# State-space scan: one wide exponential per chunk, with the tokens' numbers added by GpSimd

## The chip, the core and the metric

The kernel runs on one core of a Trainium2 chip. A core has five engines that run side by side, each with its own in-order queue: TensorE (PE, matrix products; PEld is its weight load), VectorE (DVE), ScalarE (ACT, activations), GpSimd (POOL), and SyncE (SP), which issues most transfers. They share the on-chip memory SBUF; matrix products land in PSUM, which PE, DVE and ACT reach. The metric is the device time of one execution in microseconds; the runs of the kernel before lie between 2413.68 and 2415.92 us.

## The reference, cut to what matters

The reference is one layer of a hybrid streaming encoder: one large input projection, a state-space branch (SSD) and an attention branch side by side, an output projection, and a convolutional feed-forward part. The change touches the scan of the state-space branch only:

```
acum = cumsum(dt * a_neg)                        # over the tokens of a chunk
seg = acum[:, :, None] - acum[:, None, :]        # token l minus token s
decay = exp(where(causal, seg, -inf))
xdt = xc * dt
cb = einsum('blgn,bsgn->blsg', cc, bc)
y = einsum('blsg,blsge,bsgep->blgep', cb, decay, xdt)
y = y + einsum('blgn,bgepn->blgep', cc, state) * exp(acum)
state = state * exp(acum[:, -1]) + einsum('blgn,blge,blgep->bgepn', bc, exp(acum[:, -1:] - acum), xdt)
```

There are 32 heads in 4 groups of 8, with 64 values a head and a state of 128. One stream of 1024 tokens and one of 64 tokens are computed together (1088 tokens). The kernel uses chunks of 128 tokens where the reference has 64, which gives the same result.

## The kernel before, in words

Everything is float32. Large matrix products are made of three products of rounded high and low halves (lines 170 to 172 in `product`); they are most of PE's work, before, during and after the scan.

The scan (function `scan`, with `ask`, `front`, `back`, `gated`, `normed`, `scaled`) runs over 4 groups and, in each, 9 chunks: eight of 128 tokens and one of 64 for the short stream, 36 steps. Step by step:

- `ask` (L1284, SP) loads a tile `bc` of 128 rows by 8 heads by 128 tokens: the cumulated decay exponents of the chunk's 8 heads, the same in every row. It has four buffers and is asked for two steps ahead.
- `front` prepares a chunk: ACT takes exp of `bc` into `e2` (L1294, two halves of 64 rows); PE transposes the inputs (`tr`, L1297) and makes the product `cb` (L1299, L1300); ACT copies that to `b_cb` (L1302); DVE scales the inputs into `xx` (L1306). Then GpSimd masks `bc` in place (L1307, the upper triangle gets -1e30), ACT takes eight exponentials, one a head, each with that head's number of the row's token (`nacum`, the negated cumulated exponent) as bias (L1309), and DVE multiplies the result with `cb` (L1310). In this tile a row is token s and a column token l, so the bias is one number a row and head.
- `back` uses it: PE multiplies the weights in `bc` with `xdt` (`yi`, L1318) and the state with the chunk's C (`ye`, L1324); DVE puts these together (L1325, L1326). The state moves on: GpSimd multiplies it with the chunk's decay (L1335), PE makes the update (`stp`, L1330), DVE adds it (L1337). The next chunk's `ye` needs that sum.
- After each span of three chunks the result is gated and normed (L1344 to L1362, DVE and ACT).

`scan` calls `front` for the next chunk before `back` for the present one. Between steps `fill` runs pieces of the `filler`: the rest of the input projection and the branch products, so that PE has the large products to do while the chain of small operations runs. A scheduler, which reorders instructions by priority and by its own estimate of durations, sets the final order on each engine; once built, that order is fixed, and an engine whose next instruction isn't ready waits.

Of the kernel before, what the change touches and what calls it, by code (L numbers as in the profile page):

```python
# [11 lines left out]
AF = mybir.ActivationFunctionType  # L12
ALU = mybir.AluOpType
# [76 lines left out]
def hybrid_layer(ctx: ExitStack, tc: tile.TileContext, xT, xt, prm, cst, rope, wvd, win, wbs, wba, wout, wup, wdn,  # L90
                 ckT, cv, st0, yT, kT, v, ssm, conv, ffn):
    nc = tc.nc
    V, S, G, PE = nc.vector, nc.scalar, nc.gpsimd, nc.tensor
    act = S.activation
# [166 lines left out]
    nacum, decs = (dq.tile([P, 9, 32], F32, name=n) for n in ("nacum", "decs"))  # L261
# [1003 lines left out]
    with (tc.tile_pool(name="sin", bufs=1) as sin, tc.tile_pool(name="sp", bufs=1) as sp,  # L1265
# [21 lines left out]
        def front(g, ch, o, bx, xs, bc):  # L1287
            L = P if ch < 8 else TS
            cs = slice(o, o + L)
            h8 = slice(8 * g, 8 * g + 8)  # L1290
            e2 = sp.tile([P, 4, P], F32, name="e2", tag="e2", bufs=3)
            for u in range(2):
                half = slice(64 * u, 64 * u + 64)
                act(e2[half, :, :L], bc.rearrange("p (j u) t -> p u j t", u=2)[half, u, :, :L], AF.Exp)  # L1294
            tr = psi.tile([P, 512], F32, name="tr", tag="tr")
            for j in range(4):
                PE.transpose(tr[:L, P * j : P * (j + 1)], xs[:, j, cs], ident)  # L1297
            cb = psi.tile([P, 512], F32, name="cb", tag="cb")
            PE.transpose(cb[:L, 0:P], bx[:, 0, cs], ident)  # L1299
            PE.matmul(cb[:L, P : P + L], bx[:, 0, cs], bx[:, 1, cs], start=True, stop=True)  # L1300
            b_cb = sp.tile([P, 2 * P], F32, name="b_cb", tag="b_cb", bufs=3)
            S.copy(b_cb[:L, : P + L], cb[:L, : P + L])  # L1302
            xx = sp.tile([P, 2, 8, 64], F32, name="xx", tag="xx", bufs=2)
            xdt, xw = xx[:, 0], xx[:, 1]
            tr3 = tr[:L].rearrange("p (e q) -> p e q", e=8).unsqueeze(1).to_broadcast([L, 2, 8, 64])
            V.tensor_tensor(out=xx[:L], in0=tr3, in1=dtt[:L, :, ch, h8].unsqueeze(3).to_broadcast([L, 2, 8, 64]), op=ALU.mult)  # L1306
            G.affine_select(bc[:L, :, :L], bc[:L, :, :L], [[0, 8], [1, L]], ALU.is_ge, -1e30, base=0, channel_multiplier=-1)  # L1307
            for e in range(8):
                act(bc[:L, e, :L], bc[:L, e, :L], AF.Exp, bias=nacum[:L, ch, 8 * g + e : 8 * g + e + 1])  # L1309
            V.tensor_tensor(out=bc[:L, :, :L], in0=bc[:L, :, :L], in1=b_cb[:L, P : P + L].unsqueeze(1).to_broadcast([L, 8, L]), op=ALU.mult)  # L1310
            return L, cs, bc, e2, b_cb, xdt, xw

# [65 lines left out]
        def scan():  # L1378
# [9 lines left out]
            def begin(n):  # L1388
                if n == len(steps):
                    return None  # L1390
                if n and n + 2 < len(steps):
                    asked.append(ask(*steps[n + 2]))
                i, g, c, w, o = steps[n]
                return front(g, (c + o) // P, o, *got[i], asked[n])
# [465 lines left out]
    for i in range(4 * len(DOWN)):  # L1860
        g, last = i // 4, i % 4 == 3 and i + 1 < 4 * len(DOWN)
# [125 lines left out]
```

## Time and profile before

| | us |
|---|---|
| median of three runs | 2413.91 |
| the profiled execution | 2411.51 |
| its span, from the first to the last instruction | 2409.7 |
| first and last mask of the scan (L1307) | 1130.1 and 1441.5 |
| first and last start of `yi` (L1318) | 1138.7 and 1467.0 |
| ACT busy in the eight small exponentials (L1309) | 87.2 |
| GpSimd busy in masks (L1307) | 44.2 |
| GpSimd busy in state products (L1335) | 46.9 |

The profile gives for each engine the time in which it executes something. A busy PE is not PE at its best, since products overlap and their ends are modelled. Rows of instruction groups read: line, engine, operation, output and inputs, shapes, count, then the time the group kept the engine busy, the mean of one in ns, and the idle time of the engine just before such instructions with what ended it. Rows of a timeline begin with start and duration in us. A wait is put down to what came last by the trace.

### The profile page before, as it was taken

The page shows a single profiled execution, that of the slowest core. Times are in us where ns is not written, and L with a number is a line of the kernel's source. Part 1 is how long each engine was busy: PE and PEld are TensorE (multiplying, and loading weights), DVE is VectorE, ACT ScalarE, POOL GpSimd, SP SyncE. Part 2 cuts the span into 40 slices and gives each one's busy share as a digit, 9 for nine tenths or more (in the row PEclk, how much of TensorE's full clock was granted, in tenths as well). Part 3 has the DMA queues.
Part 4 walks back from the last instruction along what each step waited for, and adds up shares of the span by engine and source line. Part 5 has one row for each costly group of instructions (what it writes and reads, how often), then busy time and mean ns, then how long its engine had stood idle before and what let it go on. Part 6 is the DMA issues. An engine that isn't in the chain of part 4 may idle for free. (4 is left out here: it accounts for less than half of the span.)

```text
span 2409.7 us, 48636 instructions
## 1 busy us (share of the span) xinstructions
PE 2373.4 (98%) x18649; PEld 2302.2 (96%) x18649; DVE 1729.4 (72%) x2938; ACT 1201.2 (50%) x2600; POOL 634.4 (26%) x689
## 2 busy tenths in 40 slices
PE   8999999999999999999999999999999999999998
PEld 8999999999999999999898889999899999999998
DVE  4678887646858768884898886647866667677765
ACT  6444454335656656665566664334443343353442
POOL 0032443320100000001223220012254455443444
PEclk9999999999999999999999999999999999999999
DMA  7873768526554444435978956663124324357876
GB/s 246 273 245 129 266 221 303 170 102 208 160 156 161 151 144 137 148 110 188 353 266 280 331 192 205 203 215 130 65 82 164 138 98 162 127 191 211 246 184 106
DMA packets 288170, 449.74 MB, mean 187 GB/s; under 512 B 35833, under 2 KB 178306, under 8 KB 287938
## 3 DMA queue, kind: packets, MB, share of 16 engines
q1 hardware_dynamic: 258594, 387.00, 48.6%
q0 software_dynamic: 11040, 26.34, 5.4%
q10 hardware_dynamic: 18304, 33.30, 3.7%
q8 instruction: 147, 2.41, 0.4%
q14 instruction: 85, 0.70, 0.1%
HBM read 294.03 MB, written 152.50 MB: 185 GB/s over the span
## 5 line engine op out<-in xcount | busy, mean ns | idle before, releaser
L170 PE MATMUL mm<-b,w_hi 128*128 128x272 f32 x1376 | 407.7, 296 | 0.0
L171 PE MATMUL mm<-b,w_hi 128*128 128x272 f32 x1376 | 405.8, 295 | 0.0
L172 PE MATMUL mm<-b,w_lo 128*128 128x272 f32 x1376 | 403.8, 294 | 0.0
L171 PEld LDWEIGHTS mm<-b,w_hi 128*128 128x128 f32 x1376 | 259.5, 189 | 5.9 <-issue 4.1
L170 PEld LDWEIGHTS mm<-b,w_hi 128*128 128x128 f32 x1376 | 259.3, 188 | 5.3 <-issue 2.7
L172 PEld LDWEIGHTS mm<-b,w_lo 128*128 128x128 f32 x1376 | 259.0, 188 | 5.2 <-issue 4.2
L1629 PE MATMUL mx<-m,w_hi 128*128 128x272 f32 x792 | 152.3, 289 | 2.5 <-DVE hb L1667 1.3
L420 DVE TENSOR_TENSOR wh<-w_f,wh 128x512 fp32r<-128x512 f32 (+1 forms) x156 | 149.7, 960 | 0.7 <-ACT wh L419 0.7
L1629 PE MATMUL mx<-n,wh 128*128 128x272 f32 x1056 | 141.7, 288 | 1.3 <-DVE u L1656 0.9
L1629 PEld LDWEIGHTS mx<-n,wh 128*128 128x128 f32 x1056 | 135.7, 188 | 1.7 <-DVE u L1656 1.2
L1132 ACT ACTIVATE p_t<-sc,mx 128x512 f32<-128x512 f32 (+6 forms) x144 | 106.0, 739 | 59.0 <-DVE mx L1123 33.0
L1629 PEld LDWEIGHTS mx<-m,w_hi 128*128 128x128 f32 x792 | 124.4, 188 | 2.9 <-DVE hb L1667 1.5
L170 PE MATMUL mx<-b,w_hi 128*128 128x272 f32 x416 | 123.4, 297 | 1.1 <-ACT w_hi L155 0.8
L172 PE MATMUL mx<-b,w_lo 128*128 128x272 f32 x416 | 121.6, 294 | 0.0
L563 POOL TENSOR_TENSOR ws<-w_f 128x512 f32<-128x512 f32 (+1 forms) x51 | 69.0, 1354 | 195.4 <-DMA w_f<-in_wdn_dram 84.2
L171 PE MATMUL mx<-b,w_hi 128*128 128x272 f32 x416 | 120.4, 290 | 0.0
L1009 DVE SCALAR_TENSOR_TENSOR cc<-pre,par,cc 128x544 f32<-128x544 f32 (+1 forms) x144 | 111.2, 772 | 8.2 <-ACT cc L1007 6.9
L156 DVE TENSOR_TENSOR w_lo<-w_f,w_hi 128x1024 fp32r<-128x1024 f32 (+1 forms) x74 | 92.5, 1251 | 33.9 <-ACT w_hi L155 33.7
L1629 PE MATMUL mx<-m,w_lo 128*128 128x272 f32 x396 | 114.2, 289 | 0.0
L1638 ACT ACTIVATE cc<-pre,par 128x544 f32<-128x544 f32 (+1 forms) x44 | 37.2, 846 | 150.0 <-DVE pre L1673 149.1
L419 ACT CAST wh<-w_f 128x512 fp32r<-128x512 f32 (+1 forms) x156 | 95.3, 613 | 26.1 <-POOL w_f L569 6.8
L155 ACT CAST w_hi<-w_f 128x1024 fp32r<-128x1024 f32 (+1 forms) x74 | 77.6, 1049 | 56.1 <-PE mm L171 30.3
(466 smaller groups left out, 7124.8 us busy)
## 6 DMA issues: line engine op xcount, KB each, us to landing
w_f<-in_win_dram SPq DMA_DIRECT2D x40, 512.0 KB, 3.9
w_f<-in_wup_dram SPq DMA_DIRECT2D x80, 256.0 KB, 2.6
w_f<-in_win_dram SPq DMA_DIRECT2D x76, 256.0 KB, 3.2
bc<-a_sc SPq DMA_DIRECT2D x32, 512.0 KB, 7.0
b<-y_sc SPq DMA_DIRECT2D x24, 544.0 KB, 8.2
h_sc<-hb SPq DMA_DIRECT2D x44, 272.0 KB, 2.1
ht<-h_sc SPq DMA_DIRECT2D x22, 544.0 KB, 4.6
t_sc<-ht SPq DMA_DIRECT2D x22, 544.0 KB, 3.0
```

What stands on the lines that cost most here:

```text
L155: S.copy(hi, w)
L156: V.tensor_tensor(out=lo, in0=w, in1=hi, op=ALU.subtract)
L170: PE.matmul(ps, a_hi, b_hi, start=i == 0, stop=False)
L171: PE.matmul(ps, a_hi, b_lo, start=False, stop=False)
L172: PE.matmul(ps, a_lo, b_hi, start=False, stop=i == n - 1)
L419: S.copy(hi, src)
L420: V.tensor_tensor(out=lo, in0=src, in1=hi, op=ALU.subtract)
L563: G.tensor_tensor(out=s1, in0=q21, in1=q22, op=ALU.add)
L1009: V.scalar_tensor_tensor(cc[:, :m], pre[:, i : i + m], cw(i), cc[:, :m], ALU.mult, ALU.add)
L1132: act(p_t[:n, :nk], sc[c][:n, :nk], AF.Exp, bias=mx[:n, c : c + 1], accum_out=dst)
L1629: PE.matmul(ps, w[x][:, c], b[y][:, k], start=start and k == i == 0, stop=k == 3 and i == 2, skip_group_check=not start)
L1638: act(cc[:, :n], pre[h][:, :n], AF.Identity, bias=col(O_FB + f), scale=cw(0))
```

## The change

GpSimd adds the tokens' numbers to the whole `bc` tile (all 8 heads, `nacum` broadcast over the columns) ahead of the mask, and ACT takes one exponential of the whole tile, without a bias. In the changed kernel the add is L1307, the mask L1308, the exponential L1309; the lines after it keep their numbers.

```diff
@@ front
             V.tensor_tensor(out=xx[:L], in0=tr3, in1=dtt[:L, :, ch, h8].unsqueeze(3).to_broadcast([L, 2, 8, 64]), op=ALU.mult)
+            G.tensor_tensor(out=bc[:L, :, :L], in0=bc[:L, :, :L], in1=nacum[:L, ch, h8].unsqueeze(2).to_broadcast([L, 8, L]), op=ALU.add)
             G.affine_select(bc[:L, :, :L], bc[:L, :, :L], [[0, 8], [1, L]], ALU.is_ge, -1e30, base=0, channel_multiplier=-1)
-            for e in range(8):
-                act(bc[:L, e, :L], bc[:L, e, :L], AF.Exp, bias=nacum[:L, ch, 8 * g + e : 8 * g + e + 1])
+            act(bc[:L, :, :L], bc[:L, :, :L], AF.Exp)
             V.tensor_tensor(out=bc[:L, :, :L], in0=bc[:L, :, :L], in1=b_cb[:L, P : P + L].unsqueeze(1).to_broadcast([L, 8, L]), op=ALU.mult)
```

The scheduler then places instructions anew from the start of the scan on. On GpSimd at the start of the scan (`state` times `decs` is the state product of L1335):

```order
 L1003 COPY conv_o<-pre 128x3
 L1004 COPY conv_o<-pre 128x3
-L1307 AFFINE_SELECT bc<-bc 128x1024 x3
-L1335 TENSOR_TENSOR state<-state,decs 128x512
-L1307 AFFINE_SELECT bc<-bc 128x1024
+L1307 TENSOR_TENSOR bc<-bc,nacum 128x1024 x2
+L1308 AFFINE_SELECT bc<-bc 128x1024 x2
+L1307 TENSOR_TENSOR bc<-bc,nacum 128x1024
+L1335 TENSOR_TENSOR state<-state,decs 128x512
+L1308 AFFINE_SELECT bc<-bc 128x1024
```

Two adds now stand ahead of the first mask, and a third add ahead of the first state product.

On ACT at the same place (`w_hi` and `gt` belong to the filler, the numbers only tell buffers apart):

```order
 L1294 ACTIVATE e_14122<-bc 64x512 x2
 L1302 COPY b_cb<-cb 128x256
-L1294 ACTIVATE e_14151<-bc 64x512 x2
+L1294 ACTIVATE e_14145<-bc 64x512 x2
 L155 CAST w_hi<-w_f 128x1024
 L970 COPY gt<-mx 128x272
-L1309 ACTIVATE bc<-bc,nacum 128x128 x8
-L1294 ACTIVATE e_14260<-bc 64x512 x2
-L1309 ACTIVATE bc<-bc,nacum 128x128 x3
-L1302 COPY b_cb<-cb 128x256
-L1309 ACTIVATE bc<-bc,nacum 128x128 x5
+L1294 ACTIVATE e_14248<-bc 64x512 x2
```

The third chunk's `e2` moves ahead of the first chunk's exponential. 

On PE shortly before the first `yi` (lines 170 to 172 are products of the filler):

```order
 L172 MATMUL mm<-b_920,w_lo 128x272
 L170 MATMUL mm<-b_920,w_hi 128x272
+L1299 MATMUL cb<-con,in 128x128
+L1300 MATMUL cb<-in 128x128
 L171 MATMUL mm<-b_921,w_hi 128x272
+L1324 MATMUL ye<-in,state 128x128 x2
+L1297 MATMUL tr<-con,in 128x128 x4
+L1324 MATMUL ye<-in,state 128x128 x2
+L1330 MATMUL stp<-xx,b_cb 128x512
```

The second chunk's `cb`, `ye` and `stp` move ahead of the first chunk's `yi`; products of the filler that stood there follow later. PE executes the same 1964 rows between its first and last row of the scan, before and after.

## The prediction

> **What bounds the kernel now.** I read the head of the page first, then the windows around the scan, then the waits of TensorE in them.
>
> ```profile
> span 2409.7 us, 48636 instructions
> PE 2373.4 (98%) x18649; PEld 2302.2 (96%) x18649; DVE 1729.4 (72%) x2938; ACT 1201.2 (50%) x2600; POOL 634.4 (26%) x689
> ```
>
> TensorE (PE) is busy for 98% of the span; all others have room on average. The change touches only the scan, so the average says little. The windows show that stage (columns: window, length, then busy time with instruction count for PE, PEld, DVE, ACT, POOL, then granted clock, DMA share, GB/s):
>
> ```profile
> 1100.00:1130.00 30.00, 29.96 (x234) 28.50 (x233) 11.48 (x20) 11.53 (x29) 1.13 (x2) 1.00 0.55 185
> 1130.00:1180.00 50.00, 50.00 (x421) 44.02 (x419) 37.12 (x44) 40.46 (x106) 18.31 (x15) 1.00 1.05 352
> 1280.00:1330.00 50.00, 48.11 (x395) 43.56 (x395) 42.86 (x62) 32.71 (x77) 14.31 (x10) 1.00 0.86 290
> 1380.00:1430.00 50.00, 48.65 (x413) 44.57 (x413) 42.42 (x51) 33.21 (x82) 13.05 (x11) 1.00 0.65 216
> 1500.00:1550.00 50.00, 49.16 (x388) 48.73 (x388) 35.91 (x77) 21.58 (x43) 0.00 (x0) 1.00 0.74 226
> 1127.00:1470.00 343.00, 339.76 (x2765) 304.35 (x2764) 284.85 (x372) 216.91 (x523) 90.78 (x68) 1.00 0.81 275
> ```
>
> Over the scan (last row) PE idles 343 - 339.8 = 3.2 us. DVE idles 58 us, ACT 126 us, POOL 252 us. The waits of PE from 1100 to 1500 us name what those 3 us are:
>
> ```profile
> PE yi L1318 <- ACT y L1328: 1.9, 1, 1.9
> PE tr L1297 <- DMA in<-x_sc: 0.7, 1, 0.7
> PE yi L1318 <- DVE y L1326: 0.6, 1, 0.6
> PE mx L170 <- ACT grs L1355: 0.3, 1, 0.3
> ```
>
> None of them is on an exponential or on GpSimd's mask. So PE's own work sets the time here, and a change to ACT and POOL moves the end only where it makes PE wait, or takes one of these waits away.
>
> **The change, part by part.** Source views of the lines it touches (min/median/max in ns), and one row for a wide pass over ACT:
>
> ```profile
> L1309 ACT ACTIVATE bc<-bc,nacum x288: 332/387/409, 1133.8 to 1445.1; 128x128 f32<-128x128 f32 x128, 64x64 f32<-64x64 f32 x16
> 1133.79 2.45 ACT L1309 ACTIVATE bc<-bc,nacum 128x128 f32<-128x128 f32 x8
> 1127.00:1470.00 343.00, 87.21 (x288) 1.00 0.81 275
> L155 ACT CAST w_hi<-w_f 128x1024 fp32r<-128x1024 f32 x17 | 17.8, 1044 | 11.3 <-PE mx L171 5.6 <-PE mm L171 5.6
> ```
>
> Exponentials. 288 small ones keep ACT busy for 87.2 us (third row: the same window, this line alone), 2.45 us for the eight of a full chunk. One pass over 128x1024 is not in the trace as an Exp; a cast of that shape takes 1.04 us. Two half-height Exps of 512 take 1.27 us together (row below), which is the upper bound; I take 1.05, since the cast has the very shape. So ACT loses 32 x 1.4 us and some 6 us for the four half chunks, about 51 us. That work lies beside PE's: ACT already idles for 126 us here, so it is worth nothing by itself.
>
> The add on GpSimd. There are 36 new tensor-tensor operations, 32 of 128x1024 and 4 of 64x512, with a broadcast operand, as the state product has at half the width:
>
> ```profile
> L1335 POOL TENSOR_TENSOR state<-state,decs x28: 1037/1047/3618, 1140.7 to 1454.3; 128x512 f32<-128x512 f32 x28
> L1335 POOL TENSOR_TENSOR state<-state,decs 128x512 f32<-128x512 f32 x28 | 42.3, 1512 | 96.5 <-DVE state L1337 77.4 <-ACT state L1333 17.4 <-PE ye L1324 1.8
> L1307 POOL TENSOR_SCALAR_AFFINE_SELECT bc<-bc x36: 652/1092/2132, 1130.1 to 1441.5; 128x1024 f32<-128x1024 f32 x32, 64x512 f32<-64x512 f32 x4
> ```
>
> Twice the width at the undisturbed 1.04 us is 2.1 us, at the mean of 1.51 us it is 3.0 us; these are the ends, and I take 2.5. POOL's work grows by 32 x 2.5 + 4 x 1.2 = 85 us, from 91 to 176 of 343 us: not the bound by sum. A chunk's path from the bc rows to the masked weights becomes 2.5 - 1.4 = 1.1 us longer. ACT's exponential waits for POOL as before; behind it in ACT's queue stand the b_cb copies and the evacuations of PSUM, which ACT's 51 freed us cover on the whole.
>
> PE. It executes the same rows in the scan, from the same first to the same last place, in another interleaving; the price is 0, and if a few groups were split more, a few tenths of a us.
>
> **What the new operation disturbs.** Here the 1.51 us mean against the 1.04 us median matters. Two rows each of POOL and DVE around 1270 us:
>
> ```profile
> 1270.30 1.09 POOL L1307 TENSOR_SCALAR_AFFINE_SELECT bc<-bc 128x1024 f32<-128x1024 f32 x1 [2.63 <-ACT e L1294]
> 1271.35 2.01 POOL L1335 TENSOR_TENSOR state<-state,decs 128x512 f32<-128x512 f32 x1
> 1261.52 0.61 DVE L1362 SCALAR_TENSOR_TENSOR y<-y,par,grs 128x384 f32<-128x384 f32 x1
> 1270.54 1.92 DVE L1310 TENSOR_TENSOR bc<-bc,b_cb 128x1024 f32<-128x1024 f32 x1
> L1310 DVE TENSOR_TENSOR bc<-bc,b_cb 128x1024 f32<-128x1024 f32 x32 | 40.5, 1265 | 9.8 <-ACT bc L1309 5.9 <-ACT b_cb L1302 3.8
> L1306 DVE TENSOR_TENSOR xx<-tr,dtt 128x1024 f32<-128x1024 f32 x32 | 38.9, 1216 | 5.3 <-PE tr L1297 3.4 <-DMA o_sc<-ol 1.8
> L156 DVE TENSOR_TENSOR w_lo<-w_f,w_hi 128x1024 fp32r<-128x1024 f32 x17 | 22.9, 1345 | 10.4 <-ACT w_hi L155 10.4
> L1362 DVE SCALAR_TENSOR_TENSOR y<-y,par,grs 128x384 f32<-128x384 f32 x32 | 21.0, 712 | 0.1
> L1344 DVE SCALAR_TENSOR_TENSOR y<-in,par,y 128x384 f32<-128x384 f32 x32 | 20.2, 690 | 0.1
> ```
>
> DVE's product of bc starts while POOL masks, and takes 1.92 us where the undisturbed shape (L1306, which reads PSUM) has 1.22: it lost 0.70 us, nearly what the mask had left (1271.39 - 1270.54 = 0.85). Then POOL's product starts within DVE's and takes 2.01 us for 1.04. So an operation of POOL and one of DVE that reads two operands from SBUF hold each other up. The groups show the toll: against 1.216 us, L1310 lost 32 x 0.05 and L156 17 x 0.13 us; against the 0.61 us row, L1362 and L1344 lost 32 x (0.10 + 0.08) us; together 9.6 us, and these are the largest groups of their kind, not all, so 10 to 18 us for POOL's 91 us. The add doubles POOL's time, and a longer operation holds longer: I take 25 us of new loss on DVE, with 10 as the lower end and 36 x 2.1 = 75 us (each add blocks for its whole length) as the upper. 25 of DVE's 58 idle us remain cover; 75 would not fit.
>
> The Trainium skill (SBUF — State Buffer, section "Who interferes with whom") says that a DVE instruction with two SBUF inputs contends with a GpSimd instruction that reads SBUF, and that the second to issue is blocked until the first ends, not slowed; these rows agree (0.70 of 0.85 us). By that rule at its worst the time is that of the third rival below; by the grouped rows it is the forecast.
>
> **Where it reaches PE.** In the first nine chunks the slack is shortest. Rows of ACT, PE and DVE:
>
> ```profile
> 1128.71 1.27 ACT L1294 ACTIVATE e<-bc 64x512 f32<-64x512 f32 x2 [1.01 <-DMA o_sc<-ol]
> 1131.27 1.27 ACT L1294 ACTIVATE e<-bc 64x512 f32<-64x512 f32 x2 [0.89 <-DMA bc<-a_sc]
> 1136.34 1.23 DVE L1310 TENSOR_TENSOR bc<-bc,b_cb 128x1024 f32<-128x1024 f32 x1 [0.34 <-ACT bc L1309]
> 1138.71 1.09 PE L1318 MATMUL yi<-bc,xx 128*64 128x128 f32 x16
> 1176.51 1.21 DVE L1310 TENSOR_TENSOR bc<-bc,b_cb 128x1024 f32<-128x1024 f32 x1
> 1178.93 1.09 PE L1318 MATMUL yi<-bc,xx 128*64 128x128 f32 x16
> 1145.23 0.68 DVE L1337 TENSOR_TENSOR state<-state,stp 128x512 f32<-128x512 f32 x1
> 1147.22 1.05 PE L1324 MATMUL ye<-in,state 128*128 128x128 f32 x8
> ```
>
> Chunk 0's weights are ready at 1137.57 and yi starts at 1138.71: 1.1 us to spare; chunk 6 has 1178.93 - 1177.72 = 1.2 us; the third chunk's ye has 1147.22 - 1145.91 = 1.3 us. Now POOL has add, add, mask, mask, add ahead of the first state product. From the end of ACT's e2 at 1130.0: adds end at 1132.6 and 1135.1, masks at 1136.2 and 1137.3, so chunk 0's weights are ready at 1136.2 + 1.05 + 1.2 = 1138.5. In the new order PE comes to yi about 1 us later than before (six products of 0.13 us fewer ahead of it, but cb, ye and stp of the next chunk more), 1139.8 by estimate: still 1.3 us to spare. The third add ends at 1139.8, the state product 1.0 to 1.7 us later, DVE's sum 0.7 us after that, at 1141.5 to 1142.2; PE comes to that ye after yi (1.1), cb (0.3) and two products, at about 1141.4. So ye waits 0.1 to 0.8 us; I take 0.7. This is the new wait: the state product now queues behind an add that it doesn't need, and what is late next is ye. The 25 us on DVE are 0.7 us a chunk; with some three chunks of the 36 that have only about 1 us to spare I put 3 x 0.7 = 2.1 us.
>
> **The sum.** The profiled execution took 2411.5 us (its span of 2409.7 and 1.8 around it). Add 0 for PE's work, 0 for ACT's 51 us, 0.7 for ye, 2.1 for late weights: 2414.3. The median of the runs shown is 2.4 us above this execution, so 2416.7, and I predict **2417 us**. Its own range is 2411 (no new wait, the 1.9 us wait gone) to 2419. About 0.2% (4.8 us) is what a measurement of this kernel can tell from no change.
>
> **The rivals.**
>
> Slower: POOL sets the pace. Mechanism: its queue is in order, and add, mask and state product of a chunk take 2.5 + 1.2 + 1.5 = 5.2 us, against a pace of (1178.9 - 1138.7) / 6 = 6.7 us in the first chunks. It decides once holds and waits for the previous state add 1.5 us a chunk. Against it: POOL's idle rows are waits for ACT and DVE that partly overlap this. For it: state products of up to 3.6 us, and 77 us of POOL's time waiting for DVE's state, behind which adds now queue. Price: nine chunks late by about 1.1 us each, 10 us: 2411.5 + 10 + 2.4 = 2424.
>
> Slower still: each add blocks DVE for its whole length. 75 us less 58 idle leaves 17 us for PE: 2431. Against it: the mean losses of DVE's groups are a tenth, not a whole operation.
>
> Faster: the freed ACT and the scan's earlier end take away all PE idle from 1100 to 1550 us: 3.2 in the scan and 0.8 in the window 1500 to 1550. 2413.9 - 4.0 = 2410. For it: the 1.9 us wait is on an ACT copy. Against it: that is all there is, so more than 4.8 us can hardly be won.
>
> The change does not do what it says: if one wide Exp takes 1.27 us or the mask goes slower on fresh sums, ACT still has room, and the time is that of the forecast.
>
> **How the numbers follow.** Forecast 0.52; POOL as the pace 0.33; full blocking 0.08; faster 0.07. The range is 2410 to 2428: it takes in the forecast, the first rival with 4 us above its price, and most of the faster case, and leaves out full blocking. Of the faster case a little over half lies beyond 0.2%, so faster 0.04, within 0.2% 0.55, slower 0.33 + 0.08 = 0.41.
>
> **What would show it.** ACT's group at L1309 should be 36 operations of about 1.05 us, ACT busy in the scan down by about 50 us. The add should be 36 operations with a mean near 2.5 us and a least value near 2.1. L1310, L1344, L1362 and L156 should have longer means, DVE busier by 10 to 40 us. PE's waits in the scan should name ye on DVE's state and yi on DVE's bc, each under 1 us, 6 us or less in all. I am wrong if PE's idle time in the scan exceeds 8 us, if the add's mean is over 3 us, or if PE's waits stand outside the scan.

## The result, and the profile after

The changed kernel takes 2429.2 us (median of six runs, 2427.6 to 2432.1), the kernel before 2414.3 us (six runs, 2410.8 to 2420.0). The ratio is 1.0061 with a 95% interval of 1.0048 to 1.0075: some 15 us slower, 12 us above the forecast of 2417 and 1.2 us above its range. The profiled execution's span is 2425.8 us, 16.1 more than before.

The head of the page after, and the windows around the scan (window, length, busy time with count for PE, PEld, DVE, ACT, POOL, then granted clock, DMA share, GB/s):

```profile
span 2425.8 us, 48419 instructions
PE 2379.5 (98%) x18649; PEld 2304.3 (95%) x18649; DVE 1759.3 (73%) x2938; ACT 1153.0 (48%) x2348; POOL 715.3 (29%) x725
```

```profile
1100.00:1130.00 30.00, 29.71 (x232) 28.24 (x232) 10.57 (x19) 11.49 (x29) 1.13 (x2) 1.00 0.51 171
1130.00:1180.00 50.00, 47.18 (x385) 40.91 (x384) 40.07 (x38) 27.18 (x45) 37.00 (x22) 1.00 1.05 345
1180.00:1230.00 50.00, 45.52 (x356) 41.30 (x356) 39.58 (x56) 21.90 (x33) 14.03 (x11) 0.97 0.86 293
1280.00:1330.00 50.00, 45.73 (x368) 40.02 (x369) 49.04 (x59) 25.81 (x39) 29.02 (x16) 1.00 0.76 245
1380.00:1430.00 50.00, 50.00 (x408) 45.06 (x406) 42.12 (x48) 26.42 (x44) 25.20 (x14) 1.00 0.78 264
1127.00:1487.00 360.00, 346.08 (x2770) 307.16 (x2770) 314.52 (x371) 169.55 (x272) 170.88 (x104) 1.00 0.80 263
```

The time went into the scan, in its first two thirds: PE idles 2.8, 4.5 and 4.3 us in the three windows of 50 us shown up to 1330 us, and nothing between 1380 and 1430. Over the scan (last row) PE idles 13.9 us, where it was 3.2. ACT fell from 216.9 to 169.6 us as worked out. GpSimd rose from 91 to 171 us. DVE rose by 30 us, though it has not one instruction more: 284.9 to 314.5. The window 1280 to 1330 has DVE at 49.0 of 50 us.

The waits of PE from 1100 to 1500 us (engine, place, what it waited for: total, times, longest):

```profile
PE mx L172 <- DVE w_lo L156: 4.1, 1, 4.1
PE gst L1352 <- DVE zin L1348: 1.8, 2, 1.0
PE cb L1299 <- ACT b_cb L1302: 1.5, 2, 1.1
PE ye L1324 <- DVE state L1337: 1.3, 1, 1.3
PE tr L1297 <- DVE y L1345: 1.2, 1, 1.2
PE yi L1318 <- DVE y L1326: 1.1, 1, 1.1
PE yi L1318 <- DVE bc L1310: 1.0, 2, 0.7
```

Six of the seven are on DVE, at six different lines: it is not one operation that grew, DVE is late in many places. Groups of DVE by shape in the scan, against those quoted before:

```profile
L1310 DVE TENSOR_TENSOR bc<-bc,b_cb 128x1024 f32<-128x1024 f32 x32 | 49.4, 1548 | 5.0 <-ACT bc L1309 4.2 <-ACT b_cb L1302 0.8
L1306 DVE TENSOR_TENSOR xx<-tr,dtt 128x1024 f32<-128x1024 f32 x32 | 38.8, 1213 | 1.9 <-DMA o_sc<-ol 1.9
L1344 DVE SCALAR_TENSOR_TENSOR y<-in,par,y 128x384 f32<-128x384 f32 x32 | 28.8, 957 | 0.1
L156 DVE TENSOR_TENSOR w_lo<-w_f,w_hi 128x1024 fp32r<-128x1024 f32 x17 | 25.1, 1476 | 7.1 <-ACT w_hi L155 7.1
L1362 DVE SCALAR_TENSOR_TENSOR y<-y,par,grs 128x384 f32<-128x384 f32 x32 | 23.3, 786 | 0.1
```

Of these five only those with two operands from SBUF are longer. L1306 reads one from PSUM and keeps its 1.21 us. Against the same marks as before (1.213 and 0.61 us) the four others lost 10.7, 11.1, 4.5 and 5.6 us, 31.9 together; it was 9.6. The timeline shows a single hold, POOL's rows first, then DVE's:

```profile
1168.59 2.60 POOL L1307 TENSOR_TENSOR bc<-bc,nacum 128x1024 f32<-128x1024 f32 x1
1171.14 1.35 POOL L1335 TENSOR_TENSOR state<-state,decs 128x512 f32<-128x512 f32 x1
1169.94 1.65 DVE L1348 TENSOR_TENSOR zin<-zin 128x384 f32<-128x384 f32 x1
1171.52 2.06 DVE L1310 TENSOR_TENSOR bc<-bc,b_cb 128x1024 f32<-128x1024 f32 x1
```

DVE's sum of 384 elements starts 1.25 us before the add ends, and ends 0.40 us after it: it hardly moved while the add ran.

### The profile page after: what moved, and what is told of

Read it like the earlier page. It is cut to its first block, busy times and chain, and to the rows that moved or that the text cites. A ratio compares the mean times of both kernels' runs of the same rounds, so it can differ in the third digit from the quotient of the medians.

```text
span 2425.8 us, 48419 instructions
## 1 busy us (share of the span) xinstructions
PE 2379.5 (98%) x18649; PEld 2304.3 (95%) x18649; DVE 1759.3 (73%) x2938; ACT 1153.0 (48%) x2348; POOL 715.3 (29%) x725
## 4 chain that ended last, share of the span: by engine, by line
PE 51%; DVE 4%; DMA 3%; issue 2%; POOL 1%; ACT 0%; SPq 0%; POOLq 0%; DVEq 0%; ACTq 0%
PE mx L1629 13%; PE mx L1803 6%; PE mm L1629 5%; PE mm L172 3%; PE mm L170 3%; PE mm L171 3%; PE mx L170 3%; PE mx L172 3%; PE mx L171 3%; PE mm L1803 2%; PE po L1167 1%; PE yi L1318 1%; PE ye L1324 1%; PE stp L1330 1%; DMA bc<-a_sc 1%
## 5 line engine op out<-in xcount | busy, mean ns | idle before, releaser
L1307 POOL TENSOR_TENSOR bc<-bc,nacum 128x1024 f32<-128x1024 f32 (+1 forms) x36 | 74.5, 2072 | 124.4 <-ACT e L1294 124.4
L1646 POOL TENSOR_TENSOR hb<-hb,cc 128x544 f32<-128x544 f32 (+2 forms) x63 | 67.1, 1079 | 133.7 <-DVE hb L1667 96.8
```

The source lines that it names most:

```text
L1307: G.tensor_tensor(out=bc[:L, :, :L], in0=bc[:L, :, :L], in1=nacum[:L, ch, h8].unsqueeze(2).to_broadcast([L, 8, L]), op=ALU.add)
```

## The experiments

Theories: **A**, GpSimd's add holds DVE's operations with two SBUF operands, DVE gets late, and PE waits for DVE. **B**, the scheduler's new order is itself worse. **C**, GpSimd's own queue is late: the longer path over add, mask and exponential, and the state product behind adds. Ratios are to runs of the kernel before on the same chip. In the last two columns stands the busy time of DVE and GpSimd, in us, from 1120 us to the end of the scan.

| kernel | ratio, 95% interval | about us | DVE | GpSimd |
|---|---|---|---|---|
| before | 1 | 0 | 287 | 91 |
| changed | 1.0061 (1.0048 to 1.0075) | +15 | 316 | 171 |
| wide_no_add | 1.0027 (1.0016 to 1.0038) | +7 | 287 | 86 |
| side_add | 1.0090 (1.0075 to 1.0106) | +22 | 322 | 171 |
| add_eight | 1.0099 (1.0083 to 1.0115) | +24 | 315 | 165 |
| add_dve | 1.0021 (1.0011 to 1.0031) | +5 | 326 | 99 |
| side_memset | 1.0005 (0.9996 to 1.0015) | +1 | 286 | 201 |
| after_state_dve | 1.0077 (1.0062 to 1.0092) | +19 | 328 | 132 |
| add_halves | 1.0079 (1.0063 to 1.0096) | +19 | 311 | 183 |
| state_dve | 1.0006 (0.9996 to 1.0017) | +1 | 296 | 43 |
| wide_memset | 1.0057 (1.0039 to 1.0076) | +14 | 289 | 162 |
| eight_no_add | 1.0045 (1.0031 to 1.0059) | +11 | 283 | 81 |
| two_no_add | 1.0015 (1.0005 to 1.0025) | +4 | 285 | 85 |
| side_copy | 1.0043 (1.0028 to 1.0058) | +10 | 310 | 181 |
| same_order_short | 1.0028 (1.0017 to 1.0039) | +7 | 286 | 95 |
| same_order_memset | 1.0033 (1.0021 to 1.0045) | +8 | 288 | 119 |
| memset_as_add | 1.0062 (1.0047 to 1.0077) | +15 | 309 | 209 |

### One part alone

The changed kernel without its add:

```diff
-            G.tensor_tensor(out=bc[:L, :, :L], in0=bc[:L, :, :L], in1=nacum[...], op=ALU.add)
             G.affine_select(bc[:L, :, :L], ...)
             act(bc[:L, :, :L], bc[:L, :, :L], AF.Exp)
```

> The changed kernel without GpSimd's add: the tokens' numbers are left out, so the decays are wrong; the wide exponential and the mask stay. Theory A (the add's hold on DVE's SBUF reads makes DVE late, and DVE makes PE late): DVE's loss falls back to its old level, PE idles 3 to 5 us in the scan, time within 0.2% of before (2410 to 2418). Theory B (the new order that the scheduler makes around one wide exponential is itself worse, by late weights for PE): still 2422 to 2430.

1.0027: between the two. DVE is back at 287 us, yet PE still waits 3.5 us for a `w_lo` and 3.0 us for ACT's copy of `grs`. So A does not cover all of it.

The kernel before with an add beside the path:

```diff
+            side_add = sp.tile([P, 8, 112], mybir.dt.bfloat16, name="side_add", tag="side_add")
+            G.tensor_tensor(out=side_add[:L, :, : min(L, 112)], in0=xx[:L]...[:, :, : min(L, 112)], in1=nacum[...], op=ALU.add)
             V.tensor_tensor(out=bc[:L, :, :L], in0=bc[:L, :, :L], in1=b_cb[...], op=ALU.mult)
```

> The kernel before (eight biased exponentials) plus one GpSimd add of 128x896 a chunk, from xx and nacum into a tile that nobody reads: the same kind of load on GpSimd, but not on the path from bc to the weights. Theory A (holding DVE up is what costs): 8 to 14 us slower than before, DVE's two-operand groups lose about as much as in the changed kernel. Theory C (the longer path from bc over add, mask and exponential to the weights is what costs): within 5 us of before.

1.0090, 22 us where A had said 8 to 14, and far from C's 5 us. The add need not be on the path to cost.

The changed kernel with narrow exponentials:

```diff
-            act(bc[:L, :, :L], bc[:L, :, :L], AF.Exp)
+            for e in range(8):
+                act(bc[:L, e, :L], bc[:L, e, :L], AF.Exp)
```

> The changed kernel with eight narrow exponentials in place of the wide one, without bias; the add on GpSimd stays. Theory A: the add does it, so 12 to 20 us slower than before, no faster than the changed kernel, since ACT's time is no bound. Theory B: order around the wide exponential is the cause, so within 5 us of before.

1.0099, 24 us where A had said 12 to 20. The add costs with narrow exponentials too; that A's figures are passed twice says that something adds to the holds (the section on order below).

The add on DVE:

```diff
-            G.tensor_tensor(out=bc[:L, :, :L], ...
+            V.tensor_tensor(out=bc[:L, :, :L], ...
```

> The changed kernel with the add on DVE instead of GpSimd: 36 more DVE operations of about 1.2 us (43 us), no new hold by GpSimd. DVE then has about 328 busy us of 343 in the scan. Theory A, which says that DVE's time is the scarce thing: 10 to 25 us slower than before, much like the changed kernel, since GpSimd's add costs DVE 27 us by holds. Theory C (GpSimd's queue, in order, is late): about as before, since GpSimd's queue is as it was.

1.0021: A's form that DVE's time as such is scarce fell. DVE is busy for 326 us, 10 more than in the changed kernel, and the kernel is 10 us faster than that one. C's forecast, about as before, was the nearer one; whether a full queue is the cause is asked next.

### What on GpSimd costs

The kernel before with memsets beside the path:

```diff
+            side_add = sp.tile([P, 8, 112], mybir.dt.bfloat16, name="side_add", tag="side_add")
+            G.tensor_copy(out=side_add[:L, 0, 0:1], in_=xx[:L, 0, 0, 0:1])
+            for _ in range(3):
+                G.memset(side_add[:L], 0.0)
             V.tensor_tensor(out=bc[:L, :, :L], in0=bc[:L, :, :L], in1=b_cb[...], op=ALU.mult)
```

> The kernel before plus, a chunk, three GpSimd memsets of a tile that nobody reads (and a one-column copy that ties them to the chunk): GpSimd's queue is about as full as with the add beside the path, but the memsets read nothing from SBUF. Theory A (the add holds DVE's two-operand reads): DVE's loss stays at 15 to 25 us and the time within 5 us of before. Theory C (GpSimd's queue gets late, whatever runs in it): 10 us slower or more, as with the add beside the path.

No change (1.0005, the interval holds 1), with the fullest GpSimd but one: 201 us. Its row in the scan, to be held against the last row of the profile after:

```profile
1127.00:1468.00 341.00, 338.86 (x2753) 302.79 (x2752) 284.64 (x370) 216.09 (x522) 201.20 (x212) 1.00 0.83 276
```

DVE has its old 284.6 us and PE idles 2.1 us. Here GpSimd's queue is more than twice as full without harm, with memsets, which read nothing from SBUF. The Trainium skill (SBUF — State Buffer, section "Who interferes with whom") says just that: a DVE instruction with two SBUF inputs contends with a GpSimd instruction that reads SBUF and not with one that only writes it. These runs agree.

The state product on DVE in the changed kernel, and in the kernel before:

```diff
-                G.tensor_tensor(out=new.rearrange("p (e q) -> p e q", e=8), in0=state.rearrange(...), ...
+                V.tensor_tensor(out=new.rearrange("p (e q) -> p e q", e=8), in0=state.rearrange(...), ...
```

> The changed kernel with the state product (L1335) on DVE, so that it no longer queues behind adds. Theory C: most of the 15 us come back, 2414 to 2420. Theory A: the adds still hold DVE and only the state product's own holds go; 5 to 15 us slower than before remain.

> The kernel before with the state product on DVE: 32 DVE operations of some 0.7 us more (22 us), GpSimd left with the masks. Theory A: DVE loses about 10 us less by holds, and the time is within 5 us of before, perhaps a little faster. If DVE's busy time as such were scarce: 5 to 15 us slower.

1.0077 and 1.0006. With nothing queued behind the adds but masks, the loss is still there: C's 2414 to 2420 falls. It is also above the 5 to 15 us that A had left. In the kernel before, 32 more operations on DVE cost nothing that can be measured, and the holds that they spare win nothing.

The add in two halves of four heads:

> The changed kernel with the add in two operations of four heads each: the same elements, holds of half the length. If the length of one hold does it: 2418 to 2424, DVE's longest products well under 2.9 us. If the sum of held time does it: 2426 to 2434, as the changed kernel.

1.0079, no better than one whole add: shorter holds were no remedy here. The two kernels differ in order too, so the 4 us between them can't be put down to the halves.

GpSimd copies that read one operand, beside the path:

```diff
+            for _ in range(2):
+                G.tensor_copy(out=side_add[:L, :, : min(L, 112)], in_=xx[:L]...[:, :, : min(L, 112)])
```

> The kernel before plus, a chunk, two GpSimd copies of 128x896 from xx to a tile that nobody reads: one operand read from SBUF where the add reads two. If any GpSimd read holds DVE: 8 to 20 us slower, DVE's loss 35 us or more. If only GpSimd's two-operand operations do: within 5 us of before, DVE's loss under 25 us.

1.0043, with DVE at 310 us for 287 before: one operand read is enough to hold DVE up.

### How much is order

> The changed kernel with the add replaced by two GpSimd memsets of a tile nobody reads, ahead of the mask (the tokens' numbers are left out, so the decays are wrong): about the same delay ahead of the mask, but nothing read from SBUF. Theory A (the add costs by holding DVE's reads): about the time of the kernel without the add, 2415 to 2421. Theory C (the delay ahead of the mask costs): 2426 to 2432.

> Eight narrow exponentials without bias and no add (the tokens' numbers are left out): the kernel before but for the bias. Theory B (the order made around one wide exponential costs some 6 us): within 3 us of before.

> Two exponentials of four heads each, no add (the tokens' numbers are left out). Theory B as a property of wide exponentials: 2 to 7 us slower than before, between eight and one. Theory B as chance (any new order may be some us better or worse): anywhere within 8 us of before, also outside those two.

(`wide_memset` puts a one-column copy of `bc` and two memsets of 128x896 where the add stood; the other two are the kernel without add with eight or two exponentials.)

1.0057, 1.0045 and 1.0015. A had wide_memset at the time without the add; that missed, and DVE's 289 us say that it isn't holds. C had it 12 to 18 us up, and 14 fit; but its order is new as well, and this run can't part a delay from an order. B's first forecast, within 3 us for eight_no_add, missed too. Without an add, eight, two and one exponential give +11, +4 and +7 us: in no order of width. So each of these changes made the scheduler place some 1600 products and the small operations anew, and such an order costs about 4 to 11 us by itself in the three kernels without an add.

To part order and holds, the order had to stay. In the next three the program is built as in a measured kernel, and only then, with all instructions and their waits in place, GpSimd's instruction in the add's place is replaced:

```diff
+    # in the finished program, for each GpSimd add bc <- bc, nacum:
+    b.instructions[k] = _short(i)                                  # same_order_short: one column
+    b.instructions[k] = _as(mybir.InstMemset, i, [], [i.outs[0]], ...)   # same_order_memset: memset of the tile
+    # memset_as_add, in side_memset's program: of three memsets of side_add
+    b.instructions[k] = _as(mybir.InstTensorTensor, i, [x, y], [o], op=ALU.add)   # the first: an add of 836, from par and nacum
+    b.instructions[k] = _short(i)                                  # the second: one column
```

> The changed kernel with every instruction in its place, but the add cut to one column (the tokens' numbers are left out): what is left against before is the new order alone. Theory A (holds make up most of the loss): 2 to 7 us slower than before. Theory B (the new order makes up most of it): 10 to 16 us slower, as the changed kernel.

1.0028: the changed kernel's order alone costs about 7 us. PE's waits in it:

```profile
PE tr L1297 <- DMA in<-x_sc: 2.4, 1, 2.4
PE mx L172 <- DVE w_lo L156: 2.4, 1, 2.4
PE cb L1299 <- ACT grs L1355: 1.8, 1, 1.8
PE cb L1299 <- ACT b_cb L1302: 1.6, 1, 1.6
```

The wait for `w_lo`, 4.1 us in the profile of the changed kernel, is 2.4 us here: more than half of it is there without the add.

> The changed kernel with every instruction in its place, but the add replaced by a memset of the same tile, about 1 us long and reading nothing (the weights become constants). Theory A: within 3 us of the kernel whose add is cut to one column. Theory C (delay ahead of the mask and of the state product): at least half way from that kernel to the changed one.

1.0033, with a memset of 0.95 us: the delay that it brings costs at most a us or so. It is half as long as the add, so it speaks for a delay of that length only. For the add's own delay there is the DVE row of L1310 above: DVE waited 4.2 us in all for the exponentials in the changed kernel, and 5.9 us before.

> The kernel before plus three memsets a chunk, every instruction in its place, but of each three memsets the first is now an add of 128x836 of two SBUF operands and the second is cut to one column: GpSimd's queue is about as full as with three memsets, the order the same. Theory A: DVE's loss rises from 18.6 to 35 us or more and the time by 8 us or more over before. If the order decides and holds don't: within 4 us of before, as with three memsets.

1.0062 against 1.0005 for the same order with memsets: some 14 us from adds in the place of memsets, in an order that costs nothing. Its row in the scan:

```profile
1127.00:1484.00 357.00, 343.98 (x2765) 305.76 (x2763) 307.10 (x371) 217.03 (x524) 209.31 (x212) 1.00 0.79 265
```

DVE is 22 us up on its twin with memsets, GpSimd's queue 8 us fuller, and PE idles 13.0 us for 2.1. The longest wait of PE is one for a load, and the trace leads it back to DVE: the load was issued only when DVE's `y` (L1348 there) was done, for which the issuing queue had waited 3.6 us.

```profile
SPq L1271 <- DVE y L1348: 3.6, 1, 3.6
1403.83 2.26 DVE y L1348 x3
1406.96 6.80 DMA in<-x_sc
PE tr L1297 <- DMA in<-x_sc: 3.6, 1, 3.6
```

GpSimd comes late as well in this run: DVE waits 6.0 us for it, where it is 0.3 us in the twin. So a part of the 14 us can be C's; in the changed kernel DVE has no such wait.

So of the changed kernel's 15 us, the order takes 1.0028, about 7 us, and what its add does in that order the rest, about 8 us; the intervals leave the first some 3 us either way and the second some 4. That the 8 us are holds in the main rests on DVE's busy time, which falls from 316 to 286 us when the add is cut away in this order, and on memset_as_add; that no part of them is the longer delay ahead of the mask is not shown. No version here beats the kernel before.

## Why the prediction failed

**The bound** was read rightly: PE's work set the time, and only waits of PE could move it.

**ACT** was right: 36 exponentials of 1.06 us (1.05 said), 47 us less work, worth nothing in time.

**The add** came near the lower end: a mean of 2.17 us for the 32 full ones, where 2.1 to 3.0 was the range and 2.5 the choice.

```profile
L1307 POOL TENSOR_TENSOR bc<-bc,nacum 128x1024 f32<-128x1024 f32 x32 | 69.4, 2170 | 110.4 <-ACT e L1294 110.4
L1307 POOL TENSOR_TENSOR bc<-bc,nacum x36: 1035/1898/4777, 1131.4 to 1461.8; 128x1024 f32<-128x1024 f32 x32, 64x512 f32<-64x512 f32 x4
L1309 ACT ACTIVATE bc<-bc x36: 630/1058/1063, 1138.5 to 1464.8; 128x1024 f32<-128x1024 f32 x32, 64x512 f32<-64x512 f32 x4
```

**DVE's loss** was right in mechanism and size: 25 us said, 30 more busy us measured, 22 of them in the four quoted groups.

**"PE ... the price is 0"** failed. The sum took the same rows in another interleaving as free. The same order with the add cut away costs 7 us: in the new order PE comes to a `w_lo`, a load or a copy of ACT before it is ready. The profile of before could not show that, and the orders printed ahead of the prediction show that rows move, not what it costs. Why this order is the worse one stays open.

**"With some three chunks of the 36 ... 3 x 0.7"** was mis-sized, the term "late weights". It put DVE's loss on the chunk's own weights alone, and its slack was measured in the first nine chunks alone, while the window from 1280 to 1330 has 4.3 of the 13.9 us in which PE idles. Even at the first chunk, where it had 1.3 us to spare, `yi` waits: two products of `bc` (L1310) take 4.86 us together there, where two undisturbed ones take 2.4.

```profile
1139.55 4.86 DVE L1310 TENSOR_TENSOR bc<-bc,b_cb 128x1024 f32<-128x1024 f32 x2 [0.95 <-ACT bc L1309]
1142.47 1.09 PE L1318 MATMUL yi<-bc,xx 128*64 128x128 f32 x16 [0.65 <-DVE bc L1310]
```

In the changed kernel `yi` waits for `bc` for only 1.0 us; PE waits for DVE at `w_lo`, `gst`, `tr`, `ye` and `yi`. What the add costs in its order is about 8 us, not the 2.1 and 0.7 of the sum. The step in error was "25 of DVE's 58 idle us remain cover": DVE still idles 45 us in the changed scan, and PE waits for it all the same, so idle time spread over the stage is no cover for an operation that is late where PE needs it. PE's idle time in the scan, 13.9 us, is past the 8 us that the prediction named as the sign of being wrong. In add_dve, some 45 us of added DVE work in place of the holds cost only 5 us; that the scheduler had placed that work is a likely reason, not a shown one.

**The new wait of ye** was right in its place: the third chunk's `ye` waits 1.3 us for DVE's `state`, and the state product had started when the third add ended; 0.7 us was said.

**The rivals.** GpSimd as the pace had a better time than the forecast (2424), but memsets that filled its queue to 201 us did nothing. Full blocking, 2431, was nearest to the measured 2429, and that is luck: a single hold can look as it said, but DVE lost 30 us and not 75, and some 7 of the 15 us are order, which it left out.

## What to carry to other kernels

Moving work to an idle GpSimd is not free where DVE works on two SBUF operands at the same time: look in the trace for DVE groups of one shape whose mean lies above their shortest, and count every GpSimd operation that reads SBUF against them. Holds can become waits of the engine that sets the time even where the held engine has idle time left; here the same work cost 5 us on the busier engine and 15 on GpSimd, each in an order of its own. And where a scheduler orders the program, treat the new order as a term of its own, with a spread taken from variants of the kernel (here 4 to 11 us), before a few us are put down to an operation.

## What the runs showed of the hardware

A wait of PE can cost more than its length. After the 4.1 us wait in the changed kernel the granted clock fell:

```profile
1185.00:1190.00 5.00, 3.73 (x24) 2.81 (x22) 5.00 (x5) 2.81 (x4) 3.17 (x3) 1.00 0.82 254
1190.00:1195.00 5.00, 1.78 (x11) 1.78 (x12) 5.00 (x8) 2.31 (x3) 0.03 (x1) 0.91 1.02 361
1195.00:1200.00 5.00, 5.00 (x33) 5.00 (x33) 5.00 (x7) 0.00 (x0) 0.00 (x0) 0.75 1.10 376
```

By these rows the drop costs 5 x 0.09 + 5 x 0.25 = 1.7 us more, an estimate. In wide_no_add a wait of 3.0 us left the clock at 1.00 while one of 3.5 us did not, and the kernel with the add cut to one column, whose longest wait is 2.4 us, has no such window. But the length of a wait doesn't decide it: in add_dve the clock fell after one of 2.8 us, in two_no_add after one of 2.2, and in add_eight after a single wait of 1.35 us (first the wait, then the windows):

```profile
1407.22 1.10 PE L1325 MATMUL ye<-in,start 128*128 128x64 f32 x8 [1.35 <-DVE y L1326]
1405.00:1408.00 3.00, 1.65 (x14) 1.43 (x14) 3.00 (x4) 3.00 (x16) 1.15 (x1) 1.00 0.17 62
1408.00:1410.00 2.00, 2.00 (x10) 1.53 (x10) 2.00 (x4) 0.42 (x3) 0.00 (x0) 0.65 1.00 283
1410.00:1412.00 2.00, 2.00 (x18) 0.93 (x16) 1.49 (x3) 0.58 (x1) 0.19 (x1) 0.50 1.04 330
```

The Trainium skill (TensorE: Matmul & The Clock Gate, section "What's actually happening") gives an idle window of about 3.4 us, after which the clock halves. The halving agrees, with 0.50 in the last row. The 3.4 us do not agree as the least length of one wait of PE, and the measurement decides; what else brings the clock down is not shown by these runs.
